# Third sums of seven-product steps outside the ring of raw weights, and the down projection's loads asked for in program order

## The chip, the cores and the metric

The kernel runs on one core of a Trainium2 chip. The metric is the device time of one execution in microseconds (us). A profile is one further execution, recorded by the hardware profiler; its times are counted from the start of the recorded span.

## The reference

One decoder layer of a hybrid trunk, in fp32, for 256 tokens behind 16 meta tokens, width 2048. What matters here is the last part, the gated feed-forward network with a causal convolution of three taps over time, and its down projection:

```python
def causal_dwconv(x, w, b):
    K = w.shape[0]
    y = lax.conv_general_dilated(x, w[:, None, :].astype(x.dtype), window_strides=(1,),
                                 padding=[(K - 1, 0)], dimension_numbers=('NWC', 'WIO', 'NWC'),
                                 feature_group_count=x.shape[-1])
    return y + b.astype(x.dtype)
...
    mix = jnp.concatenate([ret, hm], axis=-1).astype(h.dtype) @ w_out.astype(h.dtype)
    h = h + mix

    u = rmsnorm(h, norm_ffn)
    up = causal_dwconv(u @ w_up.astype(u.dtype), ffn_conv_w, ffn_conv_b)
    gate, val = jnp.split(up, [FFN_DIM], axis=-1)
    return h + (jax.nn.silu(gate) * val) @ w_down.astype(h.dtype)
```

`ret` and `hm` are the retention and mLSTM heads, `FFN_DIM` is 5632, `w_up` is 2048 x 11264 and `w_down` 5632 x 2048. A final rmsnorm with a gain follows.

## The kernel before

**Precision.** TensorE multiplies in a rounded fp32 form, so every fp32 weight tile is split: the raw tile is cast on ScalarE to `whi`, and VectorE forms `wlo = raw - whi`. Activations are kept as such pairs too (`mh`/`ml` for plain products, `sh`/`sl` for the sums below). A product is three matmuls: hi·hi, hi·lo and lo·hi. `load_w` (line 115) does this for a plain tile: one load of 512 KB on SyncE's queue (line 118), the cast (line 121), the difference (line 123). The raw tiles are a ring of four buffers called `wraw`; `whi` and `wlo` are rings of five.

**The FFN in two halves.** The loop over `half` first makes 22 pairs of columns of the up projection (gate and value, 128 x 258 matmuls of lines 130 to 133), then the down projection of this half. Each projection's result goes through `conv3` (line 677, one scaling, one activation and two multiply-adds, into a tile `gt` or `vt`), the gate through SiLU, and gate times value is split into the down projection's operands. `gt` and `vt` have two buffers each in the pool `wk2`.

**The down projection.** A half has two passes, b = 0 and b = 2, each over a pair of blocks of 512 output columns. A pass has 11 steps q = 0 to 10. Each step covers two 128-row tiles of `w_down`.
- Plain steps (q = 0, 4, 9, 10; in the last pass 7 and 8 as well): `load_step` (line 911) loads and splits a tile for each block of columns, and `product` (line 814) gives 12 matmuls of 128 x 512 for each of the two, 24 in all, lines 827 to 830.
- Fast steps (the others): `seven` (line 832) does the 2 x 2 block product with seven products rather than eight. It loads a sum made earlier (`kept`, 256 KB, line 840) and three blocks (768 KB, line 841) into one of two areas of the tile `hT`, in turn. VectorE forms two further sums from them, `ta` (128 x 1024, line 844) and `tb` (128 x 512, line 845). These "third sums" take a buffer each of the ring `wraw`, the ring in which the plain loads land. Four weight tiles are then split (lines 764 and 766): blocks 2 and 3, blocks 0 and 1, `ta`, `tb`. Twenty-one matmuls follow (lines 859, 860, 862).

At a pass's end `share` (line 880) combines the four accumulators of the fast products (`mmps`), and line 951 copies the four of the plain kind (`atps`) into buffers that GpSimd's queue adds to the residual by DMA. In the very last pass, `add` (line 898) adds the accumulators to `hn` directly, in the final norm's code (`squares`, `gather`, `finish`).

**What sets the order.** The code is written as a straight program; a list scheduler then orders each engine's instructions by their dependencies and the buffers of the rings. The loads on SyncE's queue are issued in the order that the scheduler gives them, each as soon as its buffer is free; a later one cannot pass an earlier one. `issue_after(x)` forces an instruction behind another in that order. After the up projection of the second half, `wk2` and the pool of the up projection's operand (`uh`, `ul`) are closed and a pool `more` is opened in their memory, for the final norm's gain and a scratch tile.

Of the kernel before, what the change touches and what calls it, by code (L numbers as in the profile page):

```python
# [10 lines left out]
F32 = mybir.dt.float32  # L11
F32R = mybir.dt.float32r
AF = mybir.ActivationFunctionType
ALU = mybir.AluOpType
PSUM = bass.MemoryType.PSUM

P = 128
DM = 2048
KT = DM // P
SEQ = 256  # L20
# [9 lines left out]
NF = FFN // P  # L30
# [53 lines left out]
def trunk(ctx: ExitStack, tc: tile.TileContext, io, out: bass.AP):  # L84
    nc = tc.nc

    def pool(name, bufs, **kw):
        return tc.tile_pool(name=name, bufs=bufs, **kw)

    consts = ctx.enter_context(pool("consts", 1, side="left"))  # L90
    wpool = ctx.enter_context(pool("wpool", 1, side="left"))
# [10 lines left out]
    def pcol(name, i, n=1):  # L102
        a = _COLS[name][0]
        return par[:, a + i : a + i + n]
# [7 lines left out]

    last_load = None

    def load_w(src, shape, to=None):
        nonlocal last_load
        raw = wpool.tile(shape, F32, name="wraw", bufs=4)
        last_load = nc.sync.dma_start(raw, src)
        to, n = (wpool, 5) if to in (None, wpool) else (to, None)
        hi = to.tile(shape, F32R, name="whi", bufs=n)  # L120
        nc.scalar.copy(hi, raw)  # L121
        lo = to.tile(shape, F32R, name="wlo", bufs=n)
        nc.vector.tensor_tensor(out=lo, in0=raw, in1=hi.bitcast(F32), op=ALU.subtract)  # L123
        return hi, lo
# [81 lines left out]
    with pool("sq", 1, side="right") as sqp:  # L206
        for k0, k1 in [(0, 1), (1, 2)] + [(k, k + 2) for k in range(2, KT, 2)]:
            n = k1 - k0
# [3 lines left out]
            raw = wpool.tile([P, 2, W0], F32, name="wraw", bufs=4)[:, :n, :]  # L212
# [3 lines left out]
            if k0 >= 2:  # L216
                last_load = load
            for k in range(k0, k1):
                nc.scalar.activation(xh[:, k, :], hT[:, k, :], AF.Copy, scale=pcol("gmix", k))
                nc.vector.scalar_tensor_tensor(out=xl[:, k, :], in0=hT[:, k, :], scalar=pcol("gmix", k),  # L220
                                               in1=xh[:, k, :].bitcast(F32), op0=ALU.mult, op1=ALU.subtract)
# [6 lines left out]
            for k in range(k0, k1):  # L228
                i = k - k0
                first, last = k == 0, k == KT - 1  # L230
                for j, (ps, t0) in enumerate(((k_ps, 0), (q_ps, TQ))):
                    w = hi[:, :, j * P : (j + 1) * P], lo[:, :, j * P : (j + 1) * P]
# [36 lines left out]
    with tc.issue_after(parted.ins):  # L269
        a = _COLS["retn"][0]  # L270
        nc.vector.tensor_scalar(out=norms[:, :RH], in0=par[:, a : a + RH], scalar1=-0.5, scalar2=None, op0=ALU.mult)

        a = _COLS["mln"][0]
# [295 lines left out]
    wk2 = wk2_cm.__enter__()  # L569
# [22 lines left out]
    NQD = NHF // 2  # L592
# [4 lines left out]
    S1, S2, S3, S4, A11, A12, A22 = range(7)  # L597
# [21 lines left out]
    early, running = {}, []  # L619
# [47 lines left out]
    def x_tile(i):  # L667
        return x5[:, i, :]
# [5 lines left out]
        for t in range(2):  # L674
            nc.vector.transpose(dst[:, :, t, 32 * i : 32 * (i + 1)], src[:, :, t, a, :])

    def conv3(ps, f, name):
        u = wk2.tile([P, NQ], F32, name="cu", bufs=1)
        nonlocal evacuated
        evacuated = nc.vector.tensor_tensor(out=u, in0=ps[:, :NQ], in1=rstd2, op=ALU.mult)  # L680
        o = wk2.tile([P, SEQ], F32, name=name)
        nc.scalar.activation(o, u[:, 2:], AF.Identity, scale=pcol("fw", 3 * f + 2), bias=pcol("fb", f))
        for j in range(2):
            nc.vector.scalar_tensor_tensor(out=o, in0=u[:, j : j + SEQ], scalar=pcol("fw", 3 * f + j), in1=o, op0=ALU.mult, op1=ALU.add)
        return o
# [53 lines left out]


    left = hT.rearrange("p k t -> p (k t)")[:, 0:4096].rearrange("p (i a n) -> i p a n", i=2, a=4)
    turn = 0

    for half in range(2):
        units = [(b, q) for b in (0, 2) for q in FAST if (half, b) != (1, 2) or q not in BOTH]
# [5 lines left out]
        else:  # L751
            begins = [2 + 38 * i // (len(units) - 1) for i in range(len(units))]
            homes = 5 * homes
            early = {}
# [13 lines left out]
        gt = None  # L768
        for jj in range(NHF):
            j = half * NHF + jj  # L770
            pair = []
            for s in range(2):
                pair.append(project(io["wu"][2 * j + s], uh, ul, 0))
                if j == 0 and s == 0:
                    norm2()
                for e in running:
                    e.age += 1
                if running and running[0].age == 2:
                    running.pop(0).finish(evacuated)
                if 2 * jj + s in begins:  # L780
                    n = begins.index(2 * jj + s)
                    b, q = units[n]
                    running.append(Early(b, half * NQD + q, homes[n], gt, pace))
                    early[b, q] = running[-1].kept
            gt = conv3(pair[0], j, "gt")
            vt = conv3(pair[1], NF + j, "vt")
            nc.scalar.activation(gt, gt, AF.Silu)
            nc.vector.tensor_tensor(out=gt, in0=gt, in1=vt, op=ALU.mult)
            q, i = divmod(jj, 2)
            if q in PLAIN:  # L790
                k = 2 * PLAIN.index(q) + i
                copied, parted = split(mh[:, k, :], ml[:, k, :], gt)
            elif i == 0:
                f = FAST.index(q)
                even = gt
                copied, parted = split(sh[:, f, A11, :], sl[:, f, A11, :], gt[:, 0:P])
            else:
                e11, e21, e12, e22 = even[:, 0:P], even[:, P:], gt[:, 0:P], gt[:, P:]
                if half == 1 and q in BOTH:
                    split(*(a[:, BOTH.index(q), :] for a in a21), e21)  # L800
                sums = x_tile(0).rearrange("p (a t) -> p a t", a=4)
                nc.gpsimd.tensor_tensor(out=sums[:, S1, :], in0=e21, in1=e22, op=ALU.add)
                nc.gpsimd.tensor_tensor(out=sums[:, S3, :], in0=e11, in1=e21, op=ALU.subtract)
                nc.gpsimd.tensor_tensor(out=sums[:, S2, :], in0=sums[:, S1, :], in1=e11, op=ALU.subtract)
                nc.gpsimd.tensor_tensor(out=sums[:, S4, :], in0=e12, in1=sums[:, S2, :], op=ALU.subtract)
                split(sh[:, f, A12:, :], sl[:, f, A12:, :], gt.rearrange("p (a t) -> p a t", a=2))
                copied, parted = split(sh[:, f, 0:4, :], sl[:, f, 0:4, :], sums)
            if 2 <= j < 18:
                with tc.issue_after(parted.ins):
                    transposed_h((j - 2) // 4, (j - 2) % 4)  # L810
# [21 lines left out]
        def seven(b, q, cs, ps, first, last, after, norm):  # L832


            nonlocal turn
            f = FAST.index(q)
            raw = left[turn]
            turn = 1 - turn

            nc.sync.dma_start(raw[:, 0, :], early[b, q])  # L840
            nc.sync.dma_start(raw[:, 1:4, :], io["wd7"][b // 2, half * NQD + q][:, 1:4, :])
            ta, tb = (wpool.tile([P, 2, 512], F32, name="wraw", bufs=4) for _ in range(2))

            nc.vector.tensor_tensor(out=ta, in0=raw[:, 0:1, :].to_broadcast([P, 2, 512]), in1=raw[:, 1:3, :], op=ALU.subtract)
            nc.vector.tensor_tensor(out=tb[:, 0, :], in0=raw[:, 3, :], in1=raw[:, 0, :], op=ALU.subtract)
            copied = None
            for w, to in (
                (raw[:, 2:4, :], ((S4, cs[0, 1], False, False), (A12, cs[0, 0], False, False))),
                (raw[:, 0:2, :], ((S2, ps[2], first, last), (A11, ps[0], first, last))),
                (ta, ((S3, ps[1], first, last), (S1, ps[3], first, last))),  # L850
                (tb[:, 0:1, :], ((A22, cs[1, 0], False, False),)),
            ):
                hi = wpool.tile([P, 2, 512], F32R, name="whi", bufs=5)
                lo = wpool.tile([P, 2, 512], F32R, name="wlo", bufs=5)
                n = len(to)
                with tc.issue_after(after.ins) if first and after else nullcontext():
                    copied, _ = split(hi[:, :n, :], lo[:, :n, :], w)
                for i, (m, o, begin, _) in enumerate(to):
                    nc.tensor.matmul(o, sh[:, f, m, :], hi[:, i, :], start=begin, stop=False)  # L859
                    nc.tensor.matmul(o, sl[:, f, m, :], hi[:, i, :], start=False, stop=False)  # L860
                for i, (m, o, _, end) in enumerate(to):
                    nc.tensor.matmul(o, sh[:, f, m, :], lo[:, i, :], start=False, stop=end)  # L862
            if norm:

                with tc.issue_after(copied.ins):
                    for g in norm:
                        squares(*g)
                reached = nc.gpsimd.tensor_tensor(out=junk[:, 0:1], in0=tb[:, 0, 0:1], in1=tb[:, 0, 0:1], op=ALU.add)
                with tc.issue_after(reached.ins):
                    for tt, _, c0, c1 in norm:  # L870
                        times_gain(tt, c0, c1)
# [30 lines left out]
        if half == 1:  # L902
# [3 lines left out]
            more = more_cm.__enter__()  # L906
            gfin = more.tile([P, DM], F32, name="gfin", bufs=1)
            nc.gpsimd.dma_start(gfin, io["gfin"])
            junk = more.tile([P, 512], F32, name="junk", bufs=1)

        def load_step(b, q, to=wpool):
            return load_w(io["wd"][b, half * NQD + q], [P, 2, 512], to)

        lag = 4
        gains = []
        emptied = None
        for b in (0, 2):
            cs = {}
# [3 lines left out]
            ps = [mm.tile([P, 512], F32, name="mmps") for _ in range(4)]  # L922
# [6 lines left out]
            for q in steps:  # L929
# [9 lines left out]
                for j in range(2):  # L939
                    if j == 1 and q in alone:  # L940
                        continue
                    w = load_step(b + j, q)
# [18 lines left out]
        if half == 1:  # L961
# [10 lines left out]
            for i in range(2):  # L972
                p = at.tile([P, 512], F32, name="atps")[:, 0:256]
# [95 lines left out]
```

## Time and profile before

| what | value |
|---|---|
| median of three runs | 1207.33 us (1207.29, 1207.33, 1207.91) |
| the profiled execution | 1207.7 us, its span 1205.9 us |
| granted TensorE clock, mean | 0.999 |
| TensorE (PE) busy | 1194.6 us, 99% of the span |
| VectorE (DVE) busy | 971.5 us, 81% |
| ScalarE (ACT) busy | 709.5 us, 59% |
| GpSimd (POOL) busy | 162.8 us, 14% |
| DMA | 263.27 MB, mean 218 GB/s |

How to read the lines below: PE is TensorE's matmuls, PEld its weight loads, DVE VectorE, ACT ScalarE, POOL GpSimd, SP or SPq SyncE and its queue of DMA issues. A timeline row gives the start, the duration, engine, line, operation, out<-in by the program's names, the shape and a count; in brackets stands how long the engine was idle before it and what it waited for. A windows row gives for a stretch its length, each engine's busy time and count, the granted clock, the share of the DMA engines and GB/s. On TensorE the passes of the down projection lie at 718 to about 832 us (first half) and 1084 to 1198 us (second half).

### The profile page before, as it was taken

The page shows a single profiled execution, that of the slowest core. Times are in us where ns is not written, and L with a number is a line of the kernel's source. Part 1 is how long each engine was busy: PE and PEld are TensorE (multiplying, and loading weights), DVE is VectorE, ACT ScalarE, POOL GpSimd, SP SyncE. Part 2 cuts the span into 40 slices and gives each one's busy share as a digit, 9 for nine tenths or more (in the row PEclk, how much of TensorE's full clock was granted, in tenths as well). Part 3 has the DMA queues.
Part 4 walks back from the last instruction along what each step waited for, and adds up shares of the span by engine and source line. Part 5 has one row for each costly group of instructions (what it writes and reads, how often), then busy time and mean ns, then how long its engine had stood idle before and what let it go on. Part 6 is the DMA issues. An engine that isn't in the chain of part 4 may idle for free.

```text
span 1205.9 us, 22794 instructions
## 1 busy us (share of the span) xinstructions
PE 1194.6 (99%) x8956; PEld 1151.2 (95%) x8956; DVE 971.5 (81%) x1444; ACT 709.5 (59%) x963; POOL 162.8 (14%) x223
## 2 busy tenths in 40 slices
PE   9999999999999999999999999999999999999997
PEld 9999999999999999999999998878999999998886
DVE  8968788766775966789889879897788778789897
ACT  8747656655656646555555557664555555556664
POOL 0100001111110311021122100202022112100232
PEclk9999999999999999999999999999999999999999
DMA  8765555666565965766766834959787777755956
GB/s 278 269 212 164 170 184 170 197 183 192 169 192 165 349 200 175 252 220 212 253 219 214 279 117 175 278 177 276 284 251 255 223 240 249 261 176 211 274 181 186
DMA packets 83004, 263.27 MB, mean 218 GB/s; under 512 B 14672, under 2 KB 18896, under 8 KB 82768
## 3 DMA queue, kind: packets, MB, share of 16 engines
q1 hardware_dynamic: 71952, 223.85, 57.0%
q0 software_dynamic: 10368, 37.11, 10.1%
q8 instruction: 70, 1.15, 0.4%
q10 hardware_dynamic: 576, 0.85, 0.2%
q14 instruction: 38, 0.31, 0.1%
HBM read 243.42 MB, written 11.27 MB: 211 GB/s over the span
## 4 chain that ended last, share of the span: by engine, by line
PE 96%; DMA 2%; DVE 1%; ACT 0%; issue 0%; SPq 0%; DVEq 0%; ACTq 0%
PE mmps L130 26%; PE mmps L131 25%; PE mmps L133 25%; PE atps L827 2%; PE atps L828 2%; PE atps L830 2%; PE mmps L860 2%; PE mmps L862 2%; PE mmps L859 2%; PE atps L862 1%; PE atps L860 1%; PE atps L859 1%; DMA hn<-x 1%; PE atps L379 1%; DMA hT<-in_wd 1%; PE atps L371 0%
## 5 line engine op out<-in xcount | busy, mean ns | idle before, releaser
L121 ACT CAST whi<-wraw 128x1024 fp32r<-128x1024 f32 x352 | 369.3, 1050 | 342.0 <-PE mmps L131 228.7
L123 DVE TENSOR_TENSOR wlo<-wraw,whi 128x1024 fp32r<-128x1024 f32 x352 | 432.3, 1230 | 72.5 <-ACT whi L121 70.0
L130 PE MATMUL mmps<-uh,whi 128*128 128x258 f32 x1408 | 346.1, 283 | 0.0
L131 PE MATMUL mmps<-ul,whi 128*128 128x258 f32 x1408 | 346.0, 283 | 0.0
L130 PEld LDWEIGHTS mmps<-uh,whi 128*128 128x128 f32 x1408 | 267.6, 190 | 0.1
L131 PEld LDWEIGHTS mmps<-ul,whi 128*128 128x128 f32 x1408 | 267.1, 190 | 0.1
L130 PE MATMUL mmps<-xh,whi 128*128 128x272 f32 (+2 forms) x864 | 219.8, 288 | 0.0
L131 PE MATMUL mmps<-xl,whi 128*128 128x272 f32 (+2 forms) x864 | 218.3, 286 | 0.0
L133 PE MATMUL mmps<-uh,wlo 128*128 128x258 f32 x1408 | 196.5, 282 | 0.0
L133 PEld LDWEIGHTS mmps<-uh,wlo 128*128 128x128 f32 x1408 | 179.9, 189 | 0.0
L131 PEld LDWEIGHTS mmps<-xl,whi 128*128 128x128 f32 x864 | 162.8, 188 | 0.0
L130 PEld LDWEIGHTS mmps<-xh,whi 128*128 128x128 f32 x864 | 162.5, 188 | 0.1
L133 PE MATMUL mmps<-xh,wlo 128*128 128x272 f32 (+2 forms) x864 | 126.7, 285 | 0.0
L133 PEld LDWEIGHTS mmps<-xh,wlo 128*128 128x128 f32 x864 | 114.2, 188 | 0.0
L680 DVE TENSOR_TENSOR cu<-mmps,rstd 128x258 f32<-128x258 f32 x88 | 37.4, 425 | 55.3 <-PE mmps L133 54.8
L764 ACT CAST whi<-hT 128x1024 fp32r<-128x1024 f32 x52 | 53.6, 1052 | 27.2 <-PE atps L828 7.3
L766 DVE TENSOR_TENSOR wlo<-hT,whi 128x1024 fp32r<-128x1024 f32 x52 | 62.1, 1220 | 4.9 <-ACT whi L764 3.7
L131 PE MATMUL mmps<-mixl,whi 128*128 128x258 f32 x256 | 63.0, 283 | 0.0
L130 PE MATMUL mmps<-mixh,whi 128*128 128x258 f32 x256 | 62.4, 282 | 0.0
L764 ACT CAST whi<-wraw 128x1024 fp32r<-128x1024 f32 (+1 forms) x52 | 43.0, 838 | 16.8 <-PE mmps L860 6.8
L766 DVE TENSOR_TENSOR wlo<-wraw,whi 128x1024 fp32r<-128x1024 f32 (+1 forms) x52 | 52.2, 1037 | 0.6 <-PE mmps L862 0.2
L827 PE MATMUL atps<-whi,mh 128*128 128x512 f32 (+1 forms) x132 | 50.9, 387 | 1.3 <-ACT whi L121 1.1
(280 smaller groups left out, 1700.1 us busy)
## 6 DMA issues: line engine op xcount, KB each, us to landing
wraw<-in_wu SPq DMA_DIRECT2D x176, 512.0 KB, 4.4
wraw<-in_wi SPq DMA_DIRECT2D x108, 512.0 KB, 4.1
hT<-in_wd SPq DMA_DIRECT2D x26, 768.0 KB, 4.7
wraw<-in_wd SPq DMA_DIRECT2D x36, 512.0 KB, 4.7
wraw<-in_wo SPq DMA_DIRECT2D x32, 512.0 KB, 4.2
x<-in_wd POOLq DMA_DIRECT2D x13, 768.0 KB, 7.0
hn<-x POOLq DMA_DIRECT2D x27, 256.0 KB, 7.9
hT<-kept SPq DMA_DIRECT2D x26, 256.0 KB, 2.9
```

What stands on the lines that cost most here:

```text
L121: nc.scalar.copy(hi, raw)
L123: nc.vector.tensor_tensor(out=lo, in0=raw, in1=hi.bitcast(F32), op=ALU.subtract)
L130: nc.tensor.matmul(ps, hi[:, k, :], xh(kk), start=kk == first, stop=False)
L131: nc.tensor.matmul(ps, hi[:, k, :], xl(kk), start=False, stop=False)
L133: nc.tensor.matmul(ps, lo[:, k, :], xh(kk), start=False, stop=kk == last)
L680: evacuated = nc.vector.tensor_tensor(out=u, in0=ps[:, :NQ], in1=rstd2, op=ALU.mult)
L764: copied = nc.scalar.copy(hi, x)
L766: return copied, nc.vector.tensor_tensor(out=lo, in0=x, in1=hi.bitcast(F32), op=ALU.subtract)
L827: nc.tensor.matmul(ps, ah[i], hi[:, i, cols], start=first and i == 0, stop=False)
L859: nc.tensor.matmul(o, sh[:, f, m, :], hi[:, i, :], start=begin, stop=False)
L860: nc.tensor.matmul(o, sl[:, f, m, :], hi[:, i, :], start=False, stop=False)
L862: nc.tensor.matmul(o, sh[:, f, m, :], lo[:, i, :], start=False, stop=end)
```

## The change

Four things are altered. `tb` and `ta` leave the ring: in the first half `ta` stays a tile of `wraw` and `tb` becomes a buffer of a new tile `both`, in the second half both are tiles of the pool `more`, two buffers each. To make that possible, `gt` and `vt` become the halves of `both`, into which `conv3` now writes. And every load of a down projection, of `seven` and of `load_step` alike, is forced behind the load that the program asked for before it, within a half.

```diff
-    def load_w(src, shape, to=None):
+    def load_w(src, shape, to=None, after=None):
         nonlocal last_load
         raw = wpool.tile(shape, F32, name="wraw", bufs=4)
-        last_load = nc.sync.dma_start(raw, src)
+        with tc.issue_after(after.ins) if after else nullcontext():
+            last_load = nc.sync.dma_start(raw, src)
...
-    def conv3(ps, f, name):
+    def conv3(ps, f, o):
...
-        o = wk2.tile([P, SEQ], F32, name=name)
...
-            gt = conv3(pair[0], j, "gt")
-            vt = conv3(pair[1], NF + j, "vt")
+            both = wk2.tile([P, 2, SEQ], F32, name="both")
+            gt = conv3(pair[0], j, both[:, 0, :])
+            vt = conv3(pair[1], NF + j, both[:, 1, :])
...
         def seven(b, q, cs, ps, first, last, after, norm):
-            nonlocal turn
+            nonlocal turn, asked
...
-            nc.sync.dma_start(raw[:, 0, :], early[b, q])
-            nc.sync.dma_start(raw[:, 1:4, :], io["wd7"][b // 2, half * NQD + q][:, 1:4, :])
-            ta, tb = (wpool.tile([P, 2, 512], F32, name="wraw", bufs=4) for _ in range(2))
+            for to, src in ((raw[:, 0, :], early[b, q]), (raw[:, 1:4, :], io["wd7"][b // 2, half * NQD + q][:, 1:4, :])):
+                with tc.issue_after(asked.ins) if asked else nullcontext():
+                    asked = nc.sync.dma_start(to, src)
+            if half == 0:
+                ta = wpool.tile([P, 2, 512], F32, name="wraw", bufs=4)
+                tb = wk2.tile([P, 2, SEQ], F32, name="both").rearrange("p a t -> p (a t)")
+            else:
+                ta, tb = more.tile([P, 2, 512], F32, name="ta"), more.tile([P, 512], F32, name="tb")
...
-            nc.vector.tensor_tensor(out=tb[:, 0, :], in0=raw[:, 3, :], in1=raw[:, 0, :], op=ALU.subtract)
+            nc.vector.tensor_tensor(out=tb, in0=raw[:, 3, :], in1=raw[:, 0, :], op=ALU.subtract)
...
         def load_step(b, q, to=wpool):
-            return load_w(io["wd"][b, half * NQD + q], [P, 2, 512], to)
-
+            nonlocal asked
+            w = load_w(io["wd"][b, half * NQD + q], [P, 2, 512], to, asked)
+            asked = last_load
+            return w
+
+        asked = None
```

The order on SyncE's queue at the change from pass b = 0 to b = 2 of the first half, before. `in_wd` with 128x1536 are the three blocks of a fast step, with 128x1024 plain tiles; the digit behind `kept` is q:

```order
L840 DMA hT<-kept_1_6644 128x512
L841 DMA hT<-in_wd 128x1536
L118 DMA wraw<-in_wd 128x1024 x2
L840 DMA hT<-kept_2_6936 128x512
L841 DMA hT<-in_wd 128x1536
L118 DMA wraw<-in_wd 128x1024 x4
L840 DMA hT<-kept_3_7228 128x512
L841 DMA hT<-in_wd 128x1536
L840 DMA hT<-kept_5_7514 128x512
L841 DMA hT<-in_wd 128x1536
L118 DMA wraw<-in_wd 128x1024 x2
```

The same place after:

```order
L119 DMA wraw<-in_wd 128x1024 x6
L843 DMA hT<-kept_1_6639 128x512
L843 DMA hT<-in_wd 128x1536
L843 DMA hT<-kept_2_6929 128x512
L843 DMA hT<-in_wd 128x1536
L843 DMA hT<-kept_3_7219 128x512
L843 DMA hT<-in_wd 128x1536
L119 DMA wraw<-in_wd 128x1024 x2
L843 DMA hT<-kept_5_7503 128x512
L843 DMA hT<-in_wd 128x1536
```

The six plain loads (q = 9 and 10 of the old pass, q = 0 of the new) now all stand ahead of the loads of steps 1 and 2, and the two of q = 4 stand ahead of step 5's instead of behind them.

VectorE at the end of the second half's up projection, before. The `cu` rows are the last convolutions, `ml` rows the splits of their results, rows of lines 844 and 845 the third sums:

```order
L766 TENSOR_TENSOR ml<-gt,mh 128x256
L684 SCALAR_TENSOR_TENSOR gt<-cu,par,gt 128x256 x2
L680 TENSOR_TENSOR cu<-mmps,rstd_78 128x258
L766 TENSOR_TENSOR wlo<-wraw,whi 128x1024
L684 SCALAR_TENSOR_TENSOR vt<-cu,par,vt 128x256 x2
L788 TENSOR_TENSOR gt<-gt,vt 128x256
L766 TENSOR_TENSOR wlo<-wraw,whi 128x512
L844 TENSOR_TENSOR wraw<-hT 128x1024
```

The same place after:

```order
L766 TENSOR_TENSOR wlo<-hT,whi 128x1024
L681 TENSOR_TENSOR cu<-mmps,rstd_78 128x258
L684 SCALAR_TENSOR_TENSOR both<-cu,par,both 128x256 x2
L789 TENSOR_TENSOR both<-both 128x256
L766 TENSOR_TENSOR ml<-both,mh 128x256
L850 TENSOR_TENSOR ta<-hT 128x1024
L851 TENSOR_TENSOR tb<-hT 128x512
L850 TENSOR_TENSOR ta<-hT 128x1024
L851 TENSOR_TENSOR tb<-hT 128x512
L766 TENSOR_TENSOR wlo<-ta,whi 128x1024
L766 TENSOR_TENSOR wlo<-tb,whi 128x512
```

The third sums of steps 1 and 2 and the splits of step 1's, which stood among the convolutions, now follow the last one.

VectorE in the final norm, before:

```order
L711 TENSOR_SCALAR frt<-ss_5848,rest 128x1
L900 TENSOR_TENSOR hn<-atps,hn 128x256
L713 SCALAR_TENSOR_TENSOR frt<-frt,fr_5852 128x1
L714 SCALAR_TENSOR_TENSOR frt<-frt,fr_5852 128x1
L723 TENSOR_SCALAR hn<-hn,frt 128x256
L723 TENSOR_SCALAR hn<-hn,frt 128x768
L721 SCALAR_TENSOR_TENSOR hn<-hn,frt,gfin 128x512
L703 TENSOR_REDUCE rest<-ss_5848 128x1
L704 TENSOR_SCALAR rest<-rest 128x1
L900 TENSOR_TENSOR hn<-atps,hn 128x256
```

The same place after:

```order
L711 TENSOR_SCALAR frt<-ss_5848,rest 128x1
L713 SCALAR_TENSOR_TENSOR frt<-frt,fr_5852 128x1
L714 SCALAR_TENSOR_TENSOR frt<-frt,fr_5852 128x1
L723 TENSOR_SCALAR hn<-hn,frt 128x256
L723 TENSOR_SCALAR hn<-hn,frt 128x768
L721 SCALAR_TENSOR_TENSOR hn<-hn,frt,gfin 128x512
L906 TENSOR_TENSOR hn<-atps,hn 128x256
L703 TENSOR_REDUCE rest<-ss_5848 128x1
L704 TENSOR_SCALAR rest<-rest 128x1
L906 TENSOR_TENSOR hn<-atps,hn 128x256
```

The first addition of 256 columns stands behind the scalings of the other half of the tokens instead of ahead of them.

More of the change, by code (lines that the diff above doesn't have):

```diff
@@ L741, in trunk @@
     left = hT.rearrange("p k t -> p (k t)")[:, 0:4096].rearrange("p (i a n) -> i p a n", i=2, a=4)
-    turn = 0
+    turn, asked = 0, None
     for half in range(2):
@@ L850, in seven @@
                 (ta, ((S3, ps[1], first, last), (S1, ps[3], first, last))),
-                (tb[:, 0:1, :], ((A22, cs[1, 0], False, False),)),
+                (tb.rearrange("p (a n) -> p a n", a=1), ((A22, cs[1, 0], False, False),)),
             ):
@@ L867, in seven @@
                         squares(*g)
-                reached = nc.gpsimd.tensor_tensor(out=junk[:, 0:1], in0=tb[:, 0, 0:1], in1=tb[:, 0, 0:1], op=ALU.add)
+                reached = nc.gpsimd.tensor_tensor(out=junk[:, 0:1], in0=tb[:, 0:1], in1=tb[:, 0:1], op=ALU.add)
                 with tc.issue_after(reached.ins):
```

## The prediction

> **What bounds the kernel now.** I read the page first (span, busy time, the chain that ended last), then the windows by stage, then TensorE's waits and its timeline where it stood.
>
> ```profile
> span 1205.9 us, 22794 instructions
> ...
> PE 1194.6 (99%) x8956; PEld 1151.2 (95%) x8956; DVE 971.5 (81%) x1444; ACT 709.5 (59%) x963; POOL 162.8 (14%) x223
> ...
> PE 96%; DMA 2%; DVE 1%; ACT 0%; issue 0%; SPq 0%; DVEq 0%; ACTq 0%
> ```
>
> TensorE bounds nearly all of it: 99% busy, 96% of the last chain. The change takes no matmul away, so it can win only what TensorE idles where the change reaches, in the four passes of the down projection (two for each half of the FFN). The windows there:
>
> ```profile
> core 0: us, PE busy (x) PEld busy (x) DVE busy (x) ACT busy (x) POOL busy (x), PEclk, DMA share, GB/s
> ...
> 780.00:800.00 20.00, 19.55 (x86) 15.70 (x85) 16.70 (x18) 12.66 (x15) 0.00 (x0) 1.00 0.64 218
> 800.00:820.00 20.00, 19.35 (x85) 15.57 (x84) 19.58 (x21) 11.39 (x13) 0.00 (x0) 1.00 0.48 160
> ...
> 1084.00:1130.00 46.00, 46.00 (x204) 37.81 (x203) 42.90 (x47) 30.61 (x35) 1.25 (x2) 1.00 0.66 235
> ...
> 1130.00:1160.00 30.00, 29.84 (x131) 24.16 (x130) 26.05 (x27) 19.04 (x24) 8.82 (x10) 1.00 0.90 253
> ```
>
> TensorE misses 0.45, 0.65 and 0.16 us there, and nothing at 1084 to 1130. The granted clock is 1.00 throughout. TensorE's waits name the lines:
>
> ```profile
> PE atps L827 <- ACT whi L121: 1.1, 2, 0.7
> ...
> PE atps L827 <- ACT x L951: 0.2, 1, 0.2
> ```
>
> Three stops, two on the cast of a plain weight tile and one on the copies that empty the accumulators. Since ends of matmuls are modelled, I size the stops by starts:
>
> ```profile
> 792.09 0.39 PE L859 MATMUL atps<-whi,sh 128*128 128x512 f32 x1
> 792.32 0.39 PE L860 MATMUL atps<-whi,sl 128*128 128x512 f32 x1
> 792.54 0.63 PE L862 MATMUL mmps<-wlo,sh 128*128 128x512 f32 x2
> 793.62 0.50 PE L827 MATMUL atps<-whi,mh 128*128 128x512 f32 x1 [0.45 <-ACT whi L121]
> 793.96 0.39 PE L828 MATMUL atps<-whi,ml 128*128 128x512 f32 x1
> ...
> 817.99 0.63 PE L862 MATMUL mmps<-wlo,sh 128*128 128x512 f32 x2
> 819.27 0.51 PE L827 MATMUL atps<-whi,mh 128*128 128x512 f32 x1 [0.65 <-ACT whi L121]
> 819.61 0.40 PE L828 MATMUL atps<-whi,ml 128*128 128x512 f32 x1
> ...
> 1138.96 1.07 PE L830 MATMUL atps<-wlo,mh 128*128 128x512 f32 x4
> 1140.19 0.50 PE L827 MATMUL atps<-whi,mh 128*128 128x512 f32 x1 [0.16 <-ACT x L951]
> 1140.52 0.39 PE L828 MATMUL atps<-whi,ml 128*128 128x512 f32 x1
> ```
>
> A 512-wide matmul starts 0.23 us after the one before it (792.09 to 792.32). Two from 792.54 end their turn at 793.00, and the next starts at 793.62: 0.62 us lost. From 817.99 it is 818.45 to 819.27, 0.82. From 1138.96, four take it to 1139.88, and 1140.19 is 0.31 later. After each stop the second matmul comes 0.34, 0.34 and 0.33 later rather than 0.23: 0.11, 0.11, 0.10 more. In all **2.07 us**, which is the whole prize.
>
> **The change part by part.** Why the stops are there, from SyncE's queue, the chain and ScalarE:
>
> ```profile
> 778.53 0.33 SPq L840 DMA_DIRECT2D hT<-kept  x1
> ...
> 788.90 0.93 SPq L118 DMA_DIRECT2D wraw<-in_wd  x2
> ...
> 805.92 0.46 SPq L841 DMA_DIRECT2D hT<-in_wd  x1
> ...
> 814.57 4.94 SPq L118 DMA_DIRECT2D wraw<-in_wd  x4
> ...
> 1125.73 15.53 SPq L118 DMA_DIRECT2D wraw<-in_wd  x6
> ...
> 788.90 3.52 DMA wraw<-in_wd
> ...
> 818.17 1.05 ACT L121 CAST whi<-wraw 128x1024 fp32r<-128x1024 f32 x1 [2.91 <-PE atps L862]
> ...
> 1138.60 1.05 ACT L121 CAST whi<-wraw 128x1024 fp32r<-128x1024 f32 x1 [1.53 <-DMA wraw<-in_wd]
> 1139.56 2.04 ACT L951 COPY x<-atps 128x512 f32<-128x512 f32 x4
> ```
>
> And VectorE's work for one fast step, with its last splits of that pass:
>
> ```profile
> 785.91 1.22 DVE L844 TENSOR_TENSOR wraw<-hT 128x1024 f32<-128x1024 f32 x1 [2.88 <-DMA hT<-in_wd]
> 787.05 0.69 DVE L845 TENSOR_TENSOR wraw<-hT 128x512 f32<-128x512 f32 x1
> 787.65 1.82 DVE L766 TENSOR_TENSOR wlo<-wraw,whi 128x1024 fp32r<-128x1024 f32 x2
> ...
> 817.34 1.82 DVE L766 TENSOR_TENSOR wlo<-wraw,whi 128x1024 fp32r<-128x1024 f32 x2
> ```
>
> *First stop.* The plain loads of q = 4 are asked for at 788.90, while the third sums of step 2 (sums at 785.91 and 787.05, split from 787.65 to about 789.4) give up their ring slots; they land 3.52 us later, and the cast of 1.05 us brings TensorE to 793.62. Afterwards their slots are the last held by a load of q = 0 and by the one sum `ta` of step 1, both split long before, and in program order they come right behind the loads that start at 778.53. At worst they run wholly behind those, which VectorE saw landed at 785.91: 1 MB at the window's 218 GB/s is 4.8 us, so 790.7 for both and about 789.4 for the first tile's cast, against 793.00. The stop goes: −0.73. What is now behind them is step 5's load, by at most those 4.8 us; its sum is wanted after the splits of step 3 and q = 4, near 795 by VectorE's pace, and it would land near 793.
>
> *Second stop.* The loads of q = 9 and 10 are asked for at 814.57, one at a time as step 7's and 8's sums are split, and the first cast starts at 818.17, 3.6 us later. Afterwards both of q = 9 follow the load at 805.92, since their slots are those of `ta` of steps 5 and 6: there near 810, for a need at 818.45. q = 10 still waits for `ta` of 7 and 8 but has another 24 × 0.23 = 5.52 us. −0.93.
>
> *Third stop.* Six loads need 15.53 us from 1125.73 for their slots; the cast at 1138.60 waits 1.53 us for one of them, and the accumulator copies queue behind it on ScalarE until 1139.56. In the second half the ring now has plain tiles only, so that load can be asked for several us sooner; one copy's wait of 1.53 goes, and it had cost 0.41 on TensorE. −0.41.
>
> *What is added.* No sum, split or byte is added: `tb` is as wide as the part that was used. VectorE's total stays; its share per step matters. A fast step costs it 1.14 + 0.60 (the sums, start to start) + 3 × 1.14 + 0.60 = 5.76 us, TensorE 21 × 0.23 = 4.83; a plain step 2 × 1.14 = 2.28 against 5.52. Steps 5 to 8 in a row so eat 4 × 0.93 = 3.7 us of VectorE's lead. The lead holds before (no stop until 817.99); TensorE comes to the end of step 8 some 0.73 us sooner afterwards, and VectorE too, since q = 4's tiles no longer hold it up. The last splits end at 817.34 + 1.74 = 819.1. I put 0 to 0.5 us for a new short wait, and take 0.15.
>
> *The start of the second half's down projection* is where the change can lose. Its rows:
>
> ```profile
> 1069.17 1.22 DVE L844 TENSOR_TENSOR wraw<-hT 128x1024 f32<-128x1024 f32 x1
> ...
> 1083.45 0.96 PE mmps L133 x8
> ...
> 1084.45 0.43 DVE L680 TENSOR_TENSOR cu<-mmps,rstd 128x258 f32<-128x258 f32 x1 [0.21 <-PE mmps L133]
> ...
> 1086.96 0.42 DVE L788 TENSOR_TENSOR gt<-gt,vt 128x256 f32<-128x256 f32 x1
> ```
>
> Before, step 1's sum is formed at 1069.17, inside the projections. Afterwards its tile lies where the projections' operand lay, so it cannot start until the last of their matmuls ends near 1084.4, and VectorE's program puts it behind the last convolution. That convolution's product starts at 1086.96; with the split of its result (about 0.35) the first sum starts at 1087.7. Both pairs of sums, 2 × 1.74, end at 1091.2, and the split of the first `ta` at 1092.35. TensorE has the plain q = 0 first, 1084.4 to 1089.9, then the two tiles of step 1 that need no sum, 12 × 0.23 = 2.76, then two hi products of `ta` and, in its new order, other work until it asks for the low part near 1094.9. Cover 2.6 us; I cost the move at nothing. Were the cover gone, the moved work (two pairs of sums 3.48, one step's two splits 1.74) would stand on TensorE: 5.2 us.
>
> *Tail.* One narrow addition on VectorE goes behind other scalings:
>
> ```profile
> 1194.88 0.42 DVE L900 TENSOR_TENSOR hn<-atps,hn 128x256 f32<-128x256 f32 x1 [0.24 <-PE atps L830]
> ...
> 1197.92 0.41 DVE L900 TENSOR_TENSOR hn<-atps,hn 128x256 f32<-128x256 f32 x1
> ```
>
> The first of these is not wanted before the last reduction, just ahead of 1197.92; moved, it can delay that by its own 0.4 at most and, as the products before it also end sooner, by nothing at least. I take 0.1.
>
> **The sum.** −0.73 − 0.93 − 0.41 + 0.15 + 0.1 = −1.8. The profiled execution took 1207.7 (span 1205.9 and 1.8 around it); the runs' median is 1207.33, 0.4 below it. 1207.33 − 1.8 = **1205.5**.
>
> [...] All stops are under 1 us and the granted clock stays at 1.00. [...]
>
> **The rivals.** (A) *The stops move, not go.* VectorE is 98% busy at 800 to 820 (19.58 of 20), so with the loads early TensorE may wait for the low parts of steps 5 to 8. If VectorE were not earlier at all, TensorE would win nothing at the first stop (0.73) and up to 0.5 less at the second: 1206.5; with none of the prize left, 1207.3. For it speaks the 19.58; against it the 2.88 us in which VectorE stood at 785.91, spare time in the same pass. (B) *Slower: the second half's start.* If `ta` comes later than 1094.9, every us later is a us on TensorE. It decides when VectorE is over 2.6 us behind my chain; with no cover at all, 1205.3 + 5.2 = 1210.5. For it: a fixed start at 1084.4 and 42.9 of 46 us busy on VectorE behind it. Against: over 8 us of TensorE's work that needs no sum. (C) *Slower: strict order.* At a change of pass, loads of fast steps stand behind up to six plain ones that wait for slots. One pair too late costs 1 MB at 218 GB/s, 4.8 us: 1210.1. Against: q = 9, 10 and 0 are 16.5 us of TensorE's work over it. (D) *More is won:* the accumulators of the tail are done sooner and the end moves too by up to 0.8: 1204.5.
>
> **How the numbers follow.** 0.2% (2.4 us) is about what a measurement of this kernel can tell from no change; the whole prize is below it. Likeliest case 0.57, with 1205.0 to 1205.9 of its own; A 0.17; B 0.10; C 0.05; D 0.11. Faster (under 1204.9): D's 0.11 and a small part of the likeliest, 0.13. Slower (over 1209.7): B and C without their partial forms, 0.12. The rest, 0.75, is same. The range 1204.6 to 1208.3 leaves out part of D and most of B and C.
>
> **What would show it.** Right: TensorE's waits on the plain cast and on the accumulator copies are gone; SyncE asks for q = 4 near 779 to 783 and q = 9 near 806; the windows at 780 to 820 read 20.00 for TensorE; at 1084 to 1100 no gap. Wrong: a wait on a low part (line 766's work) in steps 5 to 8 is A; the same some 10 us after 1084 is B; a wait of VectorE on a fast load behind a pass change, passed on to TensorE, is C; an end that moves forward by clearly more than TensorE's gaps is D.

## The result and the profile after

The changed kernel takes 1226.31 us (median of 4, 1224.14 to 1229.46) against 1207.55 us: a ratio of 1.0157, 95% interval 1.0135 to 1.018. Forecast were 1205.5 us and a range of 1204.6 to 1208.3; slower had a chance of 0.12.

The page, then TensorE's waits, then the windows (length, busy time of PE, PEld, DVE, ACT and POOL, granted clock, DMA share, GB/s):

```profile
span 1224.4 us, 22790 instructions
...
PE 1199.4 (98%) x8956; PEld 1152.3 (94%) x8956; DVE 968.4 (79%) x1444; ACT 704.8 (58%) x963; POOL 167.1 (14%) x223
```

```profile
PE atps L828 <- ACT x L961: 5.5, 3, 3.4
PE atps L868 <- DVE wlo L766: 4.8, 1, 4.8
...
PE mmps L868 <- DVE wlo L766: 0.8, 2, 0.5
```

```profile
718.00:780.00 62.00, 58.71 (x252) 45.95 (x250) 54.16 (x62) 35.08 (x41) 3.55 (x4) 1.00 0.59 194
780.00:832.00 52.00, 50.97 (x221) 41.57 (x222) 46.87 (x48) 33.29 (x39) 5.16 (x6) 1.00 0.73 217
...
1084.00:1110.00 26.00, 26.00 (x135) 22.23 (x134) 22.99 (x29) 16.33 (x21) 0.53 (x1) 1.00 0.54 201
...
1140.00:1170.00 30.00, 23.14 (x88) 17.80 (x87) 18.38 (x19) 12.93 (x17) 6.67 (x9) 0.89 0.79 223
```

The two waits on plain casts are gone, as forecast. New ones stand where the passes change, near 777 us and from 1146 to 1160 us. Nothing is lost at 1084 to 1110. TensorE's timeline at the two places:

```profile
776.97 0.63 PE L831 MATMUL atps<-wlo,mh 128*128 128x512 f32 x2
781.00 0.50 PE L828 MATMUL atps<-whi,mh 128*128 128x512 f32 x1 [3.40 <-ACT x L961]
...
1154.19 0.40 PE L866 MATMUL mmps<-whi,sl 128*128 128x512 f32 x1
1159.37 1.22 PE L868 MATMUL atps<-wlo,sh 128*128 128x512 f32 x2 [4.79 <-DVE wlo L766]
1160.39 0.63 PE L865 MATMUL mmps<-whi,sh 128*128 128x512 f32 x1
1160.82 0.63 PE L866 MATMUL mmps<-whi,sl 128*128 128x512 f32 x1
```

By starts of matmuls, as in the prediction, the first half now loses 2.2 us in small stops before 762 (low parts late), 3.7 at 777 and 0.3 at 818. The second loses 2.6 in two stops on accumulator copies, 5.0 at 1154, 2.7 in the slow clock behind that (0.50 granted from 1159.4 to 1165.0, starts 0.43 us apart until 1164.9), and 0.4 near the end. That is 16.9 against 2.1 before. The last matmuls start at 1212.30 instead of 1197.30, and from there to the end it is 12.1 us instead of 8.6. So 15.0 + 3.5 make the 18.5 us between the spans.

What the stops wait for stands on three engines at the change of pass in the second half. SyncE's queue, VectorE, ScalarE, after:

```profile
1120.49 15.23 SPq L119 DMA_DIRECT2D wraw<-in_wd  x6
1135.82 1.28 SPq L843 DMA_DIRECT2D hT<-kept  x1
...
1139.76 0.33 SPq L843 DMA_DIRECT2D hT<-kept  x1
1140.14 0.44 SPq L843 DMA_DIRECT2D hT<-in_wd  x1
```

```profile
1136.41 0.69 DVE L892 TENSOR_TENSOR x<-mmps,x 128x512 f32<-128x512 f32 x1
...
1141.74 0.68 DVE L901 TENSOR_TENSOR x<-x,mmps 128x512 f32<-128x512 f32 x1
...
1156.36 1.22 DVE L850 TENSOR_TENSOR ta<-hT 128x1024 f32<-128x1024 f32 x1 [8.58 <-DMA hT<-in_wd]
```

```profile
1147.97 0.58 ACT L961 COPY x<-atps 128x512 f32<-128x512 f32 x1 [3.85 <-DMA hn<-x]
1150.44 0.58 ACT L961 COPY x<-atps 128x512 f32<-128x512 f32 x1 [1.89 <-DMA hn<-x]
```

And the same sums of `share` on VectorE before:

```profile
1129.36 0.69 DVE L886 TENSOR_TENSOR x<-mmps,x 128x512 f32<-128x512 f32 x1
...
1131.53 0.68 DVE L895 TENSOR_TENSOR x<-x,mmps 128x512 f32<-128x512 f32 x1
```

Two things are late. The last sum of `share` starts some 10 us later (1141.74 against 1131.53). Of these, 4.6 us are the first half's losses, since the second half's down projection starts at 1088.83 instead of 1084.25; the other 5.6 us arise here. The residual's DMAs that read the x tiles follow the sums, and the copies need three of these tiles. And the fast loads of steps 1 and 2 are asked for only behind six plain loads that take 15.23 us to get their slots. VectorE then stands 8.58 us for one of them, the load of 1140.14: it lands some 16 us after it is asked for, where the median of its kind on the page is 5.8 us, and the DMA engines' share is 1.05 from 1137 to 1157. The first comes from VectorE's program, which the scheduler wrote in another order: before, the four sums stood together behind two plain splits, now

```order
L124 TENSOR_TENSOR wlo<-wraw,whi 128x1024 x3
L892 TENSOR_TENSOR x_5849<-mmps,x_5849 128x512
L124 TENSOR_TENSOR wlo<-wraw,whi 128x1024
L893 TENSOR_TENSOR x_5849<-mmps,x_5849 128x512
L124 TENSOR_TENSOR wlo<-wraw,whi 128x1024
L895 TENSOR_TENSOR x_5849<-x_5849,mmps 128x512
L901 TENSOR_TENSOR x_5849<-x_5849,mmps 128x512
```

so each sum waits for the load and cast of the plain tile ahead of it.

### The profile page after: what moved, and what is told of

Same layout as the page of the kernel before. It is cut to its first block, busy times and chain, and to the rows that moved or that the text cites. A ratio compares the mean times of both kernels' runs of the same rounds, so it can differ in the third digit from the quotient of the medians.

```text
span 1224.4 us, 22790 instructions
## 1 busy us (share of the span) xinstructions
PE 1199.4 (98%) x8956; PEld 1152.3 (94%) x8956; DVE 968.4 (79%) x1444; ACT 704.8 (58%) x963; POOL 167.1 (14%) x223
## 5 line engine op out<-in xcount | busy, mean ns | idle before, releaser
L684 DVE SCALAR_TENSOR_TENSOR both<-cu,par,both 128x256 f32<-128x256 f32 x176 | 84.8, 482 | 6.0 <-ACT both L682 3.8
L682 ACT ACTIVATE both<-cu,par 128x256 f32<-128x256 f32 x88 | 53.0, 602 | 47.5 <-DVE cu L681 35.6
```

## The experiments

Two theories stood at first: the *queue theory* (the forced order of loads) and the *vector-order theory* (`share`'s sums behind late plain splits). A ratio is to the kernel before, run on the same chip.

**The ring without the forced order.** Edit:

```diff
-                with tc.issue_after(asked.ins) if asked else nullcontext():
+                with nullcontext():
...
-            w = load_w(io["wd"][b, half * NQD + q], [P, 2, 512], to, asked)
+            w = load_w(io["wd"][b, half * NQD + q], [P, 2, 512], to)
```

> The change without the forced order of loads: third sums out of the ring, loads as the scheduler orders them (fast loads of the next pass ahead of most plain ones, as in the kernel before). VectorE's program, however, still has the share's four sums split up among the splits of later plain tiles, as in the changed kernel. Queue theory (the whole loss comes from fast and plain loads standing behind one another on SyncE's queue): 1205 to 1208 us. Vector-order theory (the loss comes from the share's sums on VectorE, which release the accumulators late, so that the accumulator copies on ScalarE wait for the residual's DMAs): 1216 to 1226 us, with the waits of TensorE on the copies still there.

Measured: 1222.85 us, 1.0136 (1.0117 to 1.0155). Its waits:

```profile
PE atps L828 <- ACT x L961: 8.7, 3, 3.3
```

All that TensorE waits for in the down projections are the copies. The forced order is not needed for most of the loss.

**The forced order without the ring.** Edit:

```diff
-            if half == 0:
-                ta = wpool.tile([P, 2, 512], F32, name="wraw", bufs=4)
-                tb = wk2.tile([P, 2, SEQ], F32, name="both").rearrange("p a t -> p (a t)")
-            else:
-                ta, tb = more.tile([P, 2, 512], F32, name="ta"), more.tile([P, 512], F32, name="tb")
+            ta, tb = (wpool.tile([P, 2, 512], F32, name="wraw", bufs=4) for _ in range(2))
+            tb = tb[:, 0, :]
```

> The forced order alone: third sums back in the ring of raw tiles, loads of the down projections in program order. VectorE has two of the share's sums ahead of the third plain split and the other two behind it, so about where the kernel before has them. Queue theory: as slow as the changed kernel or slower, 1224 to 1232 us, since plain loads now wait for the slots of third sums as well and hold the fast loads behind them. Vector-order theory: 1207 to 1213 us.

Measured: 1219.99 us, 1.0106 (1.009 to 1.0122). Neither theory's number; the order costs by itself, though less than the queue theory said.

**The changed kernel with the sums together.** Edit in `load_w`, with `shared` the last sum of `share`, from the third plain tile behind it on:

```diff
-        nc.vector.tensor_tensor(out=lo, in0=raw, in1=hi.bitcast(F32), op=ALU.subtract)
+        with tc.issue_after(shared.ins) if shared and count >= 2 else nullcontext():
+            nc.vector.tensor_tensor(out=lo, in0=raw, in1=hi.bitcast(F32), op=ALU.subtract)
```

> The changed kernel in full, order of loads and ring included, but the split of a plain tile from the third on after the last fast step is forced behind the share's four sums on VectorE, so that these stand together as in the kernel before. Queue theory: the stop of VectorE on the fast load in the last change of pass (8.6 us) stays, 1220 to 1227 us. Vector-order theory: the accumulators are emptied some 10 us earlier, the waits of TensorE on the copies go, 1206 to 1212 us. Both at work in series: about 1213 to 1220.

Measured: 1216.47 us, 1.0078 (1.006 to 1.0096). Some 10 us go, some 9 stay: both work in series. TensorE's two longest waits in the down projections, and ScalarE at the first half's change of pass:

```profile
PE atps L829 <- ACT x L966: 3.7, 2, 2.7
PE mmps L869 <- DVE wlo L767: 2.3, 4, 0.9
```

```profile
777.86 0.58 ACT L966 COPY x<-atps 128x512 f32<-128x512 f32 x1 [4.30 <-DMA hn<-x]
```

So with the sums early, TensorE still waits most for the copies, and they for x tiles that the residual's DMAs read.

**The kernel before with the sums late.** Edit, with `los` the list of plain splits, whose last two are those of q = 10; the call of `share` moves behind that step, where they are known:

```diff
-            nc.vector.tensor_tensor(out=x6, in0=p6, in1=x1, op=ALU.add)
-            nc.vector.tensor_tensor(out=x7, in0=p7, in1=x6, op=ALU.add)
+            with tc.issue_after(los[-2].ins) if not final else nullcontext():
+                nc.vector.tensor_tensor(out=x6, in0=p6, in1=x1, op=ALU.add)
+            with tc.issue_after(los[-1].ins) if not final else nullcontext():
+                nc.vector.tensor_tensor(out=x7, in0=p7, in1=x6, op=ALU.add)
```

> The kernel before, its ring and its order of loads, but in the three passes that are not the last the first of the share's sums on VectorE is forced behind the split of the third plain tile and the second behind the fourth, as they stand in the changed kernel. Queue theory: within 1 us of the kernel before, 1207 to 1208.5. Vector-order theory: slower by most of the loss, 1215 to 1225 us, with TensorE waiting for the accumulator copies.

Measured: 1219.05 us, 1.0100 (1.0084 to 1.0116), with the orders of SyncE and GpSimd the same as before. Two rows of its ScalarE, and TensorE's wait:

```profile
1145.38 0.59 ACT L956 COPY x<-atps 128x512 f32<-128x512 f32 x1 [1.68 <-DMA hn<-x]
1152.16 0.59 ACT L956 COPY x<-atps 128x512 f32<-128x512 f32 x1 [6.19 <-DMA hn<-x]
```

```profile
PE atps L828 <- ACT x L956: 8.5, 2, 5.0
```

The place of two 0.6 us sums, and of the two that need their results, costs 11 us in a kernel that is otherwise the one before.

**The same, with other buffers for the copies of the second half.**

```diff
-                        x = x_tile((4, 3, 1, 0)[2 * j + n])
+                        x = more.tile([P, 512], F32, name=f"own{2 * j + n}", bufs=1) if half == 1 else x_tile((4, 3, 1, 0)[2 * j + n])
```

> The kernel before with the share's sums late on VectorE (the kernel that took 1219), and in the second half the four accumulator copies go to buffers of their own in place of the x tiles that the share's sums have just filled. If the late sums cost time because the copies must wait until the residual's DMAs have read those x tiles, the stop of 5.2 us in the second half and the slow clock behind it (7.2 us together) go and the 5.5 us of the first half stay: 1211 to 1213.5. If the copies wait for ScalarE's own order or for the loads, 1218 to 1220 as before.

Measured: 1212.26 us, 1.0043 (1.0029 to 1.0057). The copies now run without a wait between them:

```profile
1143.26 2.05 ACT L956 COPY own<-atps 128x512 f32<-128x512 f32 x4
```

In the first half the copies keep their x tiles, and TensorE still waits 3.3 us for one of them. So what the late sums cost is the wait of the copies for x tiles that the residual's DMAs still read. That step is shown for the second half.

**The ring with the sums together and the loads free.** The edits of the first and third experiment in one.

> Third sums out of the ring, the loads free as the scheduler orders them (no forced order), and the plain splits from the third on behind the share's four sums on VectorE. If the two causes found so far are all (the share's sums behind late plain splits, 10 us; the forced order of loads, the other 8), both are gone here, and what was predicted of the ring comes out: 1204.5 to 1207. If taking the third sums out of the ring costs something of its own (sums that start late in the second half, VectorE behind in runs of fast steps), 1210 to 1214, with waits of TensorE on low parts.

Measured: 1210.32 us, 1.0024 (1.0015 to 1.0033). At the lower end of the second expectation, with the waits on low parts that it names (1.3 us): 16 of 19 us are gone, and the ring, with the sums held together, costs some 2.9 (1.8 to 4.0). Against the third experiment the forced order costs 6.2. The fast loads of the last pass, here and there:

```profile
1120.30 0.33 SPq L844 DMA_DIRECT2D hT<-kept  x1
...
1126.05 0.33 SPq L844 DMA_DIRECT2D hT<-kept  x1
...
1130.66 11.04 SPq L119 DMA_DIRECT2D wraw<-in_wd  x6
```

```profile
1119.55 15.04 SPq L119 DMA_DIRECT2D wraw<-in_wd  x6
1134.68 0.39 SPq L844 DMA_DIRECT2D hT<-kept  x1
...
1139.70 0.52 SPq L844 DMA_DIRECT2D hT<-kept  x1
```

With free loads (first fence) the two steps' loads are asked for some 14 us sooner, some 10 if counted from the start of the second half's down projection (1083.38 here, 1087.62 there). VectorE starts step 2's sum at 1132.28 without a wait, there at 1156.59. At the first half's change of pass the copies there wait 4.30, 1.02 and 0.63 us for the residual's DMAs, the first until 777.86, 9.6 us after the first of these DMAs is issued (768.27); here TensorE waits 0.2 us for copies in all. That the loads which come late come together, and that the crowding slows these DMAs, is a reading of the rows; no run changes it alone.

**The forced order starting anew at step 1 of each pass**, with ring and sums as in the third experiment:

```diff
+                    if q == fast[0]:
+                        asked = None
```

> The kernel with the changed ring, the forced order of loads and the share's sums early (1216.5 us), but the forced order starts anew at step 1 of each pass, so that the first fast loads of a pass may be asked for ahead of the six plain loads that wait for slots; within a pass the order stays. If the cost of the forced order (1216.5 less 1210.3, 6.2 us) lies at the change of pass, it goes: 1209.5 to 1211.5. If it lies in the order within a pass, 1215 to 1217.

Measured: 1211.71 us, 1.0040 (1.0027 to 1.0053). Most of the 6.2 us (4.8) lie at the change of pass: the third experiment's waits on the copies are gone in both halves, while one of 1.7 us on a plain cast near the end has come.

**The forced order on the old ring, sums together.** The edits of the second and third experiment in one.

> The forced order of loads alone, on the ring of the kernel before (third sums in it), with the share's sums early on VectorE: the missing case of the three factors. If the order costs the same with either ring (6.2 us with the new one), 1212.5 to 1215. If it costs more on the old ring, since plain loads then wait for third sums as well and hold the fast loads behind them longer, 1216 to 1220, as slow as the forced order with the sums half early (1220.0). If the order costs only together with the new ring, 1207 to 1209.

Measured: 1220.76 us, 1.0109 (1.0092 to 1.0126): 13.7 us above the kernel before. On the old ring the order costs twice as much, since the plain loads ahead wait for third sums too: the six of the last change of pass are asked for from 1130.01 on, in the third experiment from 1119.55. It is as slow as the second experiment, so on that ring the sums' place hardly matters beside the order.

**Search for a version that gains.** The ring in the first half only, the second half's as before, sums together, own buffers for the copies (edits of the sixth and fifth experiment, and):

```diff
-                ta, tb = more.tile([P, 2, 512], F32, name="ta"), more.tile([P, 512], F32, name="tb")
+                ta = wpool.tile([P, 2, 512], F32, name="wraw", bufs=4)
+                tb = wpool.tile([P, 2, 512], F32, name="wraw", bufs=4)[:, 0, :]
```

> A version made from the findings: the change's ring in the first half only (the sums' second part in the tile of gate and value), no forced order of loads, the second half's ring as before, plain splits from the third on behind the share's sums, and in the second half own buffers for the accumulator copies. If the ring's gain is real where the fast loads stay ahead and the share's sums stay early, the stops of the first half shrink from 1.7 to about 0.9 us and that of the second half goes: 1205.5 to 1206.8. If the ring in itself costs (the version with the ring in both halves was 2.9 us slower than the kernel before), 1208 to 1210.

Measured: 1209.77 us, 1.0029 (1.0018 to 1.0040). No stop in the first half, but one of 2.9 us in the last pass on a plain cast. With the last pass's splits free:

```diff
                             shared = share(ps, b, final)
+                            shared = None if final else shared
```

> The version with the changed ring in the first half only (1209.8 us), but in the last pass the plain splits are free again, with the share's sums between them as in the kernel before. Its first half had no stop at all; its loss was one stop of 2.9 us on a late plain cast near the end of the last pass, where the forced splits hold back the ring. If that rule in the last pass is the cause, the stop goes and what is left is the first half's gain: 1205 to 1206.5. If the changed first half costs elsewhere, 1208 to 1210.

Measured: 1208.74 us, 1.0013 (1.0004 to 1.0023). That is the second expectation: the stop is gone, but another of 1.3 us on the copies at 775 came. The same line in the sixth experiment, with the ring in both halves:

> The version with the changed ring in both halves, no forced order of loads and the share's sums early (1210.3 us), but in the last pass the plain splits are free again, as the scheduler had them in the changed kernel: four plain splits ahead of the share and its sums between the others. If the ring itself costs (VectorE behind with the sums of the last pass, waits on low parts of 1.9 us), 1209.5 to 1213. If the 2.9 us over the kernel before came from the forced splits, 1206 to 1208.

Measured: 1212.33 us, 1.0047 (1.0035 to 1.0059). The profile has the low parts of the last pass late, 1.9 us with their followers, as in the kernel with the forced splits:

```profile
PE mmps L869 <- DVE wlo L767: 1.4, 2, 0.9
```

Its last matmuls start 10.7 us ahead of the end, 2.1 more than in the kernel before: with the last pass free the sums are late there again. That execution, 1209.9, was the shortest of its six, so what the others lose beyond it is open. The kernel before with only the copies' buffers:

> The kernel before with one edit: in the second half the four accumulator copies go to own buffers in place of x tiles. In the kernel before they waited for a cast and its load, not for the residual's DMAs, so by the theory nothing of the third stop goes: within 0.5 us of the kernel before. If the x tiles were what holds them there too, 0.4 us less.

Measured: 1206.62 us, 0.9997 (0.9989 to 1.0006): no difference. No version beat the kernel before. This run tells something else. Up to the second half's copies its engines' programs are the same as before's, yet in its profile the first stop is missing and the second is small:

```profile
792.99 0.62 PE L862 MATMUL mmps<-wlo,sh 128*128 128x512 f32 x2
793.45 0.39 PE L827 MATMUL atps<-whi,mh 128*128 128x512 f32 x1
...
817.71 0.62 PE L862 MATMUL mmps<-wlo,sh 128*128 128x512 f32 x2
818.33 0.50 PE L827 MATMUL atps<-whi,mh 128*128 128x512 f32 x1
```

793.45 follows at the plain pace; at 818.33 and behind it 0.27 us are lost. So the first two stops that the change was to remove differ between two executions, 1.66 us in the kernel before and 0.27 us here.

## Why the prediction was wrong

- *The prize, 2.07 us.* Sized right for the execution shown, and the waits on plain casts did go. But it was one execution: with the same program the first two stops were 1.66 us once and 0.27 us once. The term was not a constant of the kernel. Nor do the changed kernel's rows bear out why the waits went: it asks for the plain loads of q = 4 at 787.92, hardly sooner than before (788.90), and TensorE comes to them at 798.53 instead of 793.62 because of its other stops. That is luck. The forecast effect shows in the kernel with ring, early sums and free loads: TensorE comes to q = 4 at 793.67 and to q = 9 at 817.93, both at the plain pace, and does not stop at either. That kernel is slower all the same, 1210.3 us.
- *"No sum, split or byte is added ... its share per step matters".* This step failed; the sum had 0.15 us for it. I counted VectorE's work and not its order at the end of a pass. With the ring free of third sums, the scheduler set plain splits ahead of `share`'s sums. Behind them the sums then waited for loads: at the second half's change of pass the last one started at 1141.74 instead of 1131.53. Price: 9.8 us in the changed kernel (1226.3 less 1216.5), 11 in the kernel before.
- *The third stop, −0.41.* I saw ScalarE's copies wait behind one cast and took that as all that could hold them. They also need x tiles back from the residual's DMAs. This second wait (3.85 and 1.89 us on ScalarE at the second half's change of pass), unseen before because the sums were early, took over.
- *Rival C, 0.05 and 4.8 us.* Fast loads did come to stand behind six plain ones that wait for slots, and at 1154 VectorE's wait for one of them passed on to TensorE, 5.0 us. The cover was wrong. I set 16.5 us of TensorE's work against it, but the slots come free when VectorE splits the plain tiles, and those splits stand behind the last fast steps: the six took 15.23 us, and the prediction's own row of the kernel before already had 15.53. The path was foreseen in part only: with the sums early, the larger wait under the forced order is on the copies (3.7 us, third experiment). Price 6.2 us on the new ring, 13.7 on the old, and it shows at the change of pass in both halves, not at one. Its chance should have been the largest of the rivals'.
- *The tail, +0.1.* It was +3.5, for the most part by the same late sums. One of the additions to `hn` waits for a residual's DMA, and all that follows on VectorE stands behind it, the narrow addition that was moved too:

```profile
1203.65 0.68 DVE L901 TENSOR_TENSOR x<-x,mmps 128x512 f32<-128x512 f32 x1
...
1209.72 0.69 DVE L906 TENSOR_TENSOR hn<-atps,hn 128x512 f32<-128x512 f32 x1 [2.46 <-DMA hn<-x]
...
1214.59 0.42 DVE L906 TENSOR_TENSOR hn<-atps,hn 128x256 f32<-128x256 f32 x1
```

  With the sums together the tail is 8.7 us (last matmuls at 1206.16 of a span of 1214.9), about that of before. The narrow addition then stands ahead of the scalings again, so that run does not part the two. By the rows the move alone is worth some 1.0 us, not 0.4 at most: ScalarE's squares of its result now come between, and the last reduction starts 1.66 us behind the start of the last scaling ahead of it (1213.92 to 1215.58) instead of 0.66 (1197.01 to 1197.67).
- *Rival B, the second half's start.* Costed at nothing, and so it was: TensorE is busy 26.00 of 26 us from 1084 on, and its first stop in the second half's down projection comes at 1147.
- *Rival A, VectorE behind.* It came in the small, 2.2 us of stops on low parts in the first pass, and remains as part of the ring's own 2.9 us.
- *The clock.* The forecast and its rivals count no slow clock. The longest stop, 5.0 us at 1154, was followed by a granted clock of 0.50 from 1159.4 to 1165.0, which cost 2.7 us more.
- *A sum* of the prediction is off by two tenths: by its own terms rival A's 1206.5 is 1206.7. It does not bear on the result.

By its parts the loss is ring 2.9, order of loads 6.2, place of the sums 9.8, in this order of adding them; the intervals leave the last two good to some 2.5 and 3.5 us. In another order the shares differ, since the new ring makes the order cheaper (13.7 to 6.2) and the sums late (12.5 us between the two kernels with free loads).

## What to carry to other kernels

Buffers freed for one kind of work also change what a list scheduler believes to be early: read every engine's program at the places where a phase ends, above all for short instructions that release other engines and now stand behind a load. A forced order of loads must be priced by when the slots of the earlier loads come free (15.23 us for six here), not by how much work lies in between. A few tenths of a per cent of stops seen in one execution are worth a second profile before they are counted as a prize.

## What the hardware showed

Stops shorter than the longest were also followed by a slow TensorE clock, and not always. In the kernel with the ring alone a wait of 2.55 us was followed by a granted clock of 0.54, in the changed kernel one of 3.40 us by 1.00. Their windows, the ring alone first:

```profile
777.00:780.30 3.30, 0.79 (x4) 0.32 (x2) 0.00 (x0) 0.59 (x2) 0.68 (x2) 1.00 1.08 189
780.30:784.00 3.70, 3.66 (x9) 2.92 (x10) 2.73 (x3) 3.70 (x5) 1.58 (x2) 0.54 0.73 129
```

```profile
777.00:781.00 4.00, 0.60 (x3) 0.16 (x1) 1.32 (x2) 0.58 (x1) 1.22 (x2) 1.00 1.09 265
781.00:785.00 4.00, 4.00 (x17) 3.30 (x18) 2.30 (x3) 2.63 (x4) 2.88 (x4) 1.00 1.13 205
```

The column behind POOL is the granted clock. A stop of 2.5 to 5 us in these runs therefore cost itself and sometimes up to 2.7 us more; what decides between the two the runs do not show.

The DMAs that add an x tile to the residual held it for some time. The eight of the second half's change of pass in the changed kernel landed 6.9 to 11.7 us after they were issued, with a median of 8.7.
